# A transpose on one core: part of the second load is shared out unevenly over the DMA engines, and VectorE waits for the last store

## The chip, the cores and the metric

The kernel runs on one core of one Trainium2 chip. The metric is the device time of one execution in microseconds (us); lower is better. Times are medians of several executions. A profile is one further execution, recorded by the hardware profiler; its span runs from the first to the last instruction.

## The reference

The output is the transpose of an 8192 x 8192 matrix of 32-bit floats, 268 MB in and 268 MB out.

```python
def setup_inputs():
    return {
        "x": np.random.randn(8192, 8192).astype(np.float32),
    }

def reference(x: np.ndarray) -> np.ndarray:
    return np.transpose(x)
```

## The kernel before

The input is cut into chunks of P = 128 rows by J = 4096 columns (S = 32 blocks of 128 x 128), 2 MB each: T = 128 chunks, first the 64 of the left half of the columns, then the 64 of the right half. A load (`load(t)`, line 101) brings chunk t into one of NIN = 3 buffers `in0` to `in2`. A row of a chunk is 4096 floats, 16 KB, and goes to one partition. Chunks 0, 1 and 2 are loaded from SyncE's queue before anything else (lines 143 and 144); every later chunk is loaded from ScalarE's queue, chunk t+3 as soon as TensorE has read chunk t.

TensorE transposes the 32 blocks of a chunk against an identity matrix (`transposes(k)`, lines 112 to 123). It writes PSUM in two halves, `ps0` and `ps1`. ScalarE copies half 0 into SBUF and VectorE copies half 1, in pieces of 128 x 512 or longer runs (line 241). A semaphore of each input buffer, `s_ld[k]`, counts 16 for a landed load and one for each of the two copying engines; TensorE waits for 18, takes 18 off and starts the next chunk. So the next chunk starts when it has landed and when both engines have copied the previous one out of PSUM. `go` in the main loop is that semaphore of the next chunk.

The copies collect in nine regions of the tensor `regs` (NREG = 9, 2 MB each). Eight regions fill at a time, each for a group of B = 4 blocks; the windows of the eight groups are staggered, so that in the steady state one region fills up with each chunk and is stored (`store(q, e, t)`, from line 154) as up to 2 MB in one transfer. Stores go out on ScalarE's queue as well: the first with the ordinary call, the others with `wide_dma` (line 25), which writes the access pattern into the instruction as it stands. Where a window runs across the change from the left to the right half of the columns, the store is cut into two pieces. A region that is used again makes the first copy into it wait for the store's semaphore `s_st[r]`. Each store adds 16 to that semaphore.

Program order on each queue sets the order of transfers. ScalarE alternates copies, a store and a load. At the end, `for r in range(NREG)` makes SyncE wait for all nine store semaphores in turn (line 266), after which all engines leave the section together.

Of the kernel before, what the change touches and what calls it, by code (L numbers as in the profile page):

```python
# [8 lines left out]
def physical(ap):  # L9


    t = ap.tensor
    dims = [list(d) for d in ap.ap]
    if len(dims) == 2:
        dims.insert(1, [dims[1][1], 1])
    return mybir.PhysicalAccessPattern(
        ap=dims,
        offset=ap.offset,
        dtype=ap.dtype,
        memref=t.name,  # L20
        memsetref=t.name + "_set",
    )


def wide_dma(nc, eng, queue, out, in_):


    return eng.add_instruction(
        mybir.InstDMACopy(
            mode="Copy",  # L30
            name=nc.get_next_instruction_name(),
            engine=eng.engine,
            ins=[physical(in_)],
            outs=[physical(out)],
            queue=queue,
        )
    )
# [3 lines left out]
def kernel(  # L41
# [13 lines left out]
    nc = tc.nc  # L55
    P = 128
# [8 lines left out]
    NIN = 3  # L65
    NREG = 9
    CH = N // P
    J = S * P

    with tc.tile_critical():  # L70
        nc.alloc_sbuf_tensor("pad", [P, 32], dt)
        ident = nc.alloc_sbuf_tensor("ident", [P, P], dt).ap()
        ins = [nc.alloc_sbuf_tensor(f"in{k}", [P, J], dt).ap() for k in range(NIN)]
        SIZE = B * W * P
# [4 lines left out]
        s_id = nc.alloc_semaphore("s_id")  # L79
        s_ld = [nc.alloc_semaphore(f"s_ld{k}") for k in range(NIN)]  # L80
        s_st = [nc.alloc_semaphore(f"s_st{k}") for k in range(NREG)]
        s_pe = nc.alloc_semaphore("s_pe")
        s_cp = [nc.alloc_semaphore("s_cpa"), nc.alloc_semaphore("s_cpv")]

# [3 lines left out]
            out=ident,  # L88
            in_=ident,
# [8 lines left out]

        chunks = [(s, c) for s in range(M // J) for c in range(CH)]

        def load(t):
            s, c = chunks[t]
            (nc.sync if t < NIN else nc.scalar).dma_start(
                out=ins[t % NIN], in_=x[c * P:(c + 1) * P, s * J:(s + 1) * J]
            ).then_inc(s_ld[t % NIN], 16)

# [34 lines left out]
        for t in range(NIN):  # L143
            load(t)

        copied = [0, 0]
        free = list(range(NREG))
        stored = [0] * NREG
        window = {}

        def later(t):
            return W <= t < T - NIN

        def store(q, e, t):
            t0, r, parts = window.pop(q)
            if later(t):
                nc.scalar.wait_ge(s_pe, (t + 1) * NH + 1)
            else:
                nc.scalar.wait_ge(s_cp[e], copied[e])
            base = 0  # L160
            pieces = []
            for s, a, z in parts:
                rows = (z - a) * P
                j0 = s * J + q * B * P
                dst = out[j0:j0 + B * P, a * P:a * P + rows]
                dst = dst.rearrange("(q b) i -> q b i", q=P)
                src = regs[:, r * SIZE + base:r * SIZE + base + B * rows]
                base += B * rows
                pieces.append((rows, dst, src))
            for rows, dst, src in sorted(pieces, key=lambda v: -v[0]):  # L170
                if any(stored):
                    st = wide_dma(nc, nc.scalar, "qActDynamicHW", dst, src)
                else:
                    st = nc.scalar.dma_start(
                        out=dst, in_=src.rearrange("q (b i) -> q b i", b=B)
                    )
                st.then_inc(s_st[r], 16)
                stored[r] += 1
            free.append(r)

        def closes(w, t):
            t0, r, parts = w
            return t + 1 == t0 + sum(z - a for _, a, z in parts)

        for t, (s, c) in enumerate(chunks):
            closed = []
            for e in range(2):
                eng = (nc.scalar, nc.vector)[e]
                go = s_ld[(t + 1) % NIN]

                place = []
                fresh = {}
                for q in range(e * NH, (e + 1) * NH):
                    if q not in window:

                        span = (q - c) % W + 1
                        r = free.pop(0)
                        parts = [(s, c, min(c + span, CH))]  # L200
                        if c + span > CH and t + span < T:
                            parts.append((s + 1, 0, c + span - CH))
                        window[q] = (t, r, parts)
                        if stored[r]:
                            fresh[q - e * NH] = (s_st[r], 16 * stored[r])
                    t0, r, parts = window[q]
                    k = [p[0] for p in parts].index(s)
                    base = r * SIZE + B * P * sum(z - a for _, a, z in parts[:k])
                    _, a, z = parts[k]
                    place.append((base + (c - a) * P, (z - a) * P))  # L210

                runs = []
                for g in range(NH):
                    if runs:
                        u = runs[-1]
                        gap = place[g][0] - place[g - 1][0]
                        if place[g][1] == place[u[0]][1] and abs(gap) < 2 ** 15 and (
                            len(u) == 1 or gap == place[u[1]][0] - place[u[0]][0]
                        ):
                            u.append(g)  # L220
                            continue
                    runs.append([g])
                if later(t):
                    runs = sorted(runs, key=lambda u: any(g in fresh for g in u))
                seen = t * NH + e * NH // 2
                for u in runs:
                    off, dist = place[u[0]]
                    gap = place[u[-1]][0] - place[u[-2]][0] if len(u) > 1 else 0
                    dims = [list(regs.ap[0]), [gap, len(u)], [dist, B], [1, P]]
                    o = bass.AP(regs.tensor, regs.offset + off, dims)  # L230
                    i = pss[e][:, u[0] * B * P:(u[-1] + 1) * B * P]
                    i = i.rearrange("p (l b i) -> p l b i", b=B, i=P)
                    need = t * NH + (e * NH + u[-1]) // 2 + 1
                    if later(t) and u is runs[0] and len(runs) > 1 and any(g in fresh for g in runs[-1]):
                        need = t * NH + (e * NH + max(v[-1] for v in runs)) // 2 + 1
                    if need > seen:
                        eng.wait_ge(s_pe, need)
                        seen = need
                    for sem, value in [fresh[g] for g in u if g in fresh]:
                        eng.wait_ge(sem, value)  # L240
                    cp = nc.scalar.copy(out=o, in_=i) if e == 0 else nc.vector.tensor_copy(out=o, in_=i)  # L241
                    ends = [e * NH + g for g in u if closes(window[e * NH + g], t)]
                    if later(t):
                        if u is runs[-1]:
                            cp.then_inc(go, 1)
                        closed += [(q, e) for q in ends]
                        continue
                    if ends:
                        cp.then_inc(s_cp[e], 1)
                        copied[e] += 1  # L250
                    if u is runs[-1]:
                        if ends:
                            eng.wait_ge(s_cp[e], copied[e])
                            eng.sem_inc(go, 1)
                        else:
                            cp.then_inc(go, 1)
                    for q in ends:
                        store(q, e, t)
            for q, e in closed:
                store(q, e, t)  # L260
            if t + NIN < T:
                if not closed:
                    nc.scalar.wait_ge(s_pe, (t + 1) * NH)
                load(t + NIN)
        for r in range(NREG):
            nc.sync.wait_ge(s_st[r], 16 * stored[r])


# [28 lines left out]
```

## Time and profile before

| | |
|---|---|
| device time, median of 3 runs | 1261.18 us (1261.06 to 1261.89) |
| span of the profiled execution | 1260.4 us |
| the profiled execution's own time | not recorded apart from its span |
| TensorE, matmul busy | 739.0 us (59%), 4096 instructions |
| VectorE busy | 302.0 us (24%), 250 instructions |
| ScalarE busy | 253.5 us (20%), 257 instructions |
| DMA | 536.95 MB, mean 426 GB/s over the span |
| queue of ScalarE (q10) | 530.60 MB, 99.0% of 16 engines' span |
| queue of SyncE (q1) | 6.29 MB, 1.2% of 16 engines' span |

Busy times say how long an engine computed, not what held the others up. The DMA row counts all bytes read and written by the core's sixteen DMA engines. A window of the trace is a stretch of the span for which the profile gives the granted TensorE clock, the mean busy share of the sixteen DMA engines and the rate in GB/s; a packet is counted in the window in which it starts.

### The profile page before, as it was taken

Reading aid. Unit: us, or ns where it says so; the run is one execution under the profiler, and the core shown is the slowest. Engines: PE = TensorE matmul, PEld = TensorE weight load, DVE = VectorE, ACT = ScalarE, POOL = GpSimd, SP = SyncE. Lnnn points to the kernel's source line nnn. Section 1 sums busy time; section 2 is a strip of 40 time slices with the busy share of each in tenths; the row PEclk is TensorE's granted clock in tenths of the full one; section 3 lists DMA queues with packets and bytes.
Section 4 is the critical chain, followed back from the end, with each engine's and each line's share of the span. In section 5 each row is a group of like instructions: output and inputs, shape, how many; then the busy total and the mean of one; then the engine's idle time right before and its main releaser. Section 6 shows DMA issues by size and latency. Waiting matters only on the chain. (4 is left out here: it accounts for less than half of the span.)

```text
span 1260.4 us, 9367 instructions
## 1 busy us (share of the span) xinstructions
PE 739.0 (59%) x4096; PEld 718.4 (57%) x4096; DVE 302.0 (24%) x250; ACT 253.5 (20%) x257; POOL 0.7 (0%) x6
## 2 busy tenths in 40 slices
PE   5656556565566655565556656566565655665561
PEld 5556556565556655565555656565565655665561
DVE  2322222222222222222222222222222222222220
ACT  3212211122111211122111211121111211121110
POOL 0000000000000000000000000000000000000000
PEclk9886876868777777778687786867777687777776
DMA  9999999999999999999999999999999999999998
GB/s 383 429 422 426 425 430 431 426 431 431 427 430 431 428 428 431 428 429 432 427 422 426 429 429 425 431 429 428 430 428 428 431 428 429 429 429 429 429 431 376
DMA packets 39271, 536.95 MB, mean 426 GB/s; under 512 B 4320, under 2 KB 4832, under 8 KB 6240
## 3 DMA queue, kind: packets, MB, share of 16 engines
q10 hardware_dynamic: 38832, 530.60, 99.0%
q1 hardware_dynamic: 432, 6.29, 1.2%
q14 instruction: 6, 0.05, 0.0%
q8 instruction: 1, 0.02, 0.0%
HBM read 268.44 MB, written 268.44 MB: 426 GB/s over the span
## 5 line engine op out<-in xcount | busy, mean ns | idle before, releaser
L117 PE MATMUL ps<-ident,in 128*128 128x128 f32 x4096 | 739.0, 362 | 493.5 <-PEq L113 493.5
L117 PEld LDWEIGHTS ps<-ident,in 128*128 128x128 f32 x4096 | 718.4, 220 | 513.9 <-issue 513.9
L241 DVE COPY regs<-ps 128x512 f32<-128x512 f32 (+3 forms) x250 | 302.0, 1246 | 932.1 <-PE ps L117 932.1
L241 ACT COPY regs<-ps 128x512 f32<-128x512 f32 (+3 forms) x256 | 252.2, 1016 | 978.8 <-PE ps L117 760.8
L241 ACT ACT_TABLE_LOAD x1 | 1.3, 1283 | 1.0 <-SPq L70 1.0
L87 POOL TENSOR_SCALAR_AFFINE_SELECT ident<-ident 128x128 f32<-128x128 f32 x1 | 0.3, 293 | 0.2 <-POOL ident L85 0.2
L85 POOL MEMSET ident<- 128x128 f32 x1 | 0.2, 204 | 0.5 <-SPq L70 0.5
L281 POOL MEMSET const-bfloat16-1.0<- 128x1 bf16 x1 | 0.1, 102 | 0.0
L281 POOL MEMSET const-uint8-127<- 128x1 uint8 x1 | 0.1, 102 | 0.0
L281 POOL MEMSET const-float32-0.0<- 128x1 f32 x1 | 0.1, 99 | 0.2 <-issue 0.2
L281 POOL MEMSET const-float32-1.0<- 128x1 f32 x1 | 0.1, 99 | 0.0
## 6 DMA issues: line engine op xcount, KB each, us to landing
in<-in_x_dram ACTq DMA_DIRECT2D x125, 2048.0 KB, 16.8
out_dram<-regs ACTq DMA_DIRECT2D x114, 2048.0 KB, 12.6
out_dram<-regs ACTq DMA_DIRECT2D x4, 1792.0 KB, 11.1
in<-in_x_dram SPq DMA_DIRECT2D x3, 2048.0 KB, 11.7
out_dram<-regs ACTq DMA_DIRECT2D x4, 1536.0 KB, 12.5
out_dram<-regs ACTq DMA_DIRECT2D x4, 1280.0 KB, 11.5
out_dram<-regs ACTq DMA_DIRECT2D x4, 1024.0 KB, 11.1
out_dram<-regs ACTq DMA_DIRECT2D x4, 768.0 KB, 12.3
```

The costliest lines, as they stand in the source:

```text
L85: nc.gpsimd.memset(ident, 0.0).then_inc(s_id, 1)
L87: nc.gpsimd.affine_select(out=ident, in_=ident, compare_op=mybir.AluOpType.not_equal, fill=1.0, base=0, pattern=[[-1, P]], channel_multipl ...
L117: tr = nc.tensor.transpose(pss[e][:, (g * B + b) * P:(g * B + b + 1) * P], ins[k][:, q * B * P + b:(q + 1) * B * P - B + b + 1:B], ident,)
L241: cp = nc.scalar.copy(out=o, in_=i) if e == 0 else nc.vector.tensor_copy(out=o, in_=i)
L281: nc = _bacc.Bacc("TRN2", target_bir_lowering=False, num_devices=1)
```

## The change

Chunk 1 is no longer loaded by one transfer. The ordinary load covers its first 112 rows. Two more transfers on SyncE's queue, made with `wide_dma`, bring the other 16: 12 rows viewed as 4 x 3 and 4 rows viewed as 2 x 2. They have a semaphore of their own, `s_ex`, and VectorE waits for 32 on it before its last copy of chunk 0, the one that reports to `s_ld[1]`. At the end of the kernel, the wait for the last region stored, `free[-1]`, is VectorE's; SyncE keeps the other eight.

```diff
     CH = N // P
     J = S * P
+    EXTRA = [(4, 3), (2, 2)]
...
         s_st = [nc.alloc_semaphore(f"s_st{k}") for k in range(NREG)]
+        s_ex = nc.alloc_semaphore("s_ex")
...
         def load(t):
             s, c = chunks[t]
+            src = x[c * P:(c + 1) * P, s * J:(s + 1) * J]
+            a = P - sum(e * n for e, n in EXTRA) if t == 1 else P
             (nc.sync if t < NIN else nc.scalar).dma_start(
-                out=ins[t % NIN], in_=x[c * P:(c + 1) * P, s * J:(s + 1) * J]
+                out=ins[t % NIN][:a], in_=src[:a]
             ).then_inc(s_ld[t % NIN], 16)
+            if t == 1:
+                for e, n in EXTRA:
+                    part = src[a:a + e * n].rearrange("(e n) j -> e n j", e=e)
+                    wide_dma(nc, nc.sync, "qSPDynamicHW", ins[t][a:a + e * n], part).then_inc(s_ex, 16)
+                    a += e * n
...
                     for sem, value in [fresh[g] for g in u if g in fresh]:
                         eng.wait_ge(sem, value)
+                    if t == 0 and e == 1 and u is runs[-1]:
+                        eng.wait_ge(s_ex, 16 * len(EXTRA))
                     cp = nc.scalar.copy(out=o, in_=i) if e == 0 else nc.vector.tensor_copy(out=o, in_=i)
...
         for r in range(NREG):
-            nc.sync.wait_ge(s_st[r], 16 * stored[r])
+            (nc.vector if r == free[-1] else nc.sync).wait_ge(s_st[r], 16 * stored[r])
```

## The prediction

> **What bounds the kernel now.** I read the page first (busy shares, slices, DMA queues), then windows over the start, the middle and the end, then the timeline of the start, the DMA issues and the waits. The page settles the bound:
>
> ```profile
> span 1260.4 us, 9367 instructions
> ## 1 busy us (share of the span) xinstructions
> PE 739.0 (59%) x4096; PEld 718.4 (57%) x4096; DVE 302.0 (24%) x250; ACT 253.5 (20%) x257; POOL 0.7 (0%) x6
> ...
> DMA  9999999999999999999999999999999999999998
> GB/s 383 429 422 426 425 430 431 426 431 431 427 430 431 428 428 431 428 429 432 427 422 426 429 429 425 431 429 428 430 428 428 431 428 429 429 429 429 429 431 376
> ```
>
> No compute engine is above 59%; the DMA engines are at nine tenths or more in every slice but the last. Windows (length, clock, DMA share, GB/s) show how completely they are filled:
>
> ```profile
> 2.00:18.00 16.00, 1.00 0.98 404
> 18.00:24.00 6.00, 1.00 1.03 394
> 24.00:60.00 36.00, 0.91 1.02 430
> 60.00:180.00 120.00, 0.78 1.01 425
> 180.00:600.00 420.00, 0.75 1.01 429
> 600.00:720.00 120.00, 0.73 1.01 426
> ```
>
> A share of 1.01 (packets overlap by a little) at 429 GB/s means that all sixteen engines work back to back: 429/16 = 26.8 GB/s each, and a row of 16 KB (4096 floats) takes 16384 B / 26.8 GB/s = 0.61 us. So the span is the work of the engine that ends last: its start, its packets at 0.61 us, its slow packets, and a tail. Bytes are equal for all sixteen, so what differs between engines is start and slow packets. The end shows by how much, if I cut it into windows of about one packet:
>
> ```profile
> 1255.20:1255.80 0.60, 0.50 1.03 437
> 1255.80:1256.40 0.60, 0.50 0.84 355
> 1256.40:1257.00 0.60, 0.50 0.65 273
> 1257.00:1257.60 0.60, 0.50 0.33 137
> 1257.60:1258.20 0.60, 0.50 0.26 109
> 1258.20:1258.80 0.60, 0.50 0.00 0
> ```
>
> GB/s times 0.6 us over 16384 B is the number of engines that begin a packet in the window: 16, 13, 10, 5, 4, 0. So after 1255.8, 3 engines begin no more packet, 3 begin one, 5 two, 1 three and 4 four. (A slow packet could hide an engine in one window; I take the counts as they are.) Perfect balance would give each 32/16 = 2 packets, so about 2 of them, 1.2 us, are all that sharing out rows could ever win here; a change in the number of slow packets comes on top.
>
> **The change, part by part.**
>
> *Rows.* Of the second load 112 rows remain in the sixteen-way transfer: 7 an engine instead of 8. Then 12 rows go to four engines (3 each) and 4 rows to two (2 each). If both small transfers start at the same engine, two engines carry 7+3+2 = 12 rows (+4), two carry 10 (+2) and twelve carry 7 (-1); bytes are conserved (8+4-12 = 0). As engines never run dry, the difference stays to the end: +2.4 us, +1.2 us and -0.6 us there. With k the packets that an engine begins after 1255.8, the last engine has 4 before; after, the two have k+4, the two others k+2, the rest k-1. The change at the end is then the largest of (k of the two), (k of the two others, minus 2) and -1, in packets. It is never below zero unless the two belong to the earliest three, and there it is about zero. This is the heart of my forecast: on these counts the moved rows can hardly win, since +4 rows uses up the whole spread of 4.
>
> The trace does not say which engines get the small transfers. [...]
>
> Any two of sixteen, drawn blindly, have as the larger k: 0 in 3 pairs of 120, 1 in 12, 2 in 40, 3 in 11, 4 in 54; the mean is (12+80+33+216)/120 = 2.8 packets, 1.7 us. Against a blind draw stands the start:
>
> ```profile
> 2.00:2.25 0.25, 1.00 1.67 328
> 2.25:2.50 0.25, 1.00 0.74 197
> 2.50:2.75 0.25, 1.00 1.13 328
> 2.75:3.00 0.25, 1.00 0.51 197
> ```
>
> By the same sum 5, 3, 5 and 3 engines take up their first packet in these four windows: the engines start one after another over some 0.9 us. If those that are served first are those that the small transfers use, they lead the mean by about 0.4 us, 0.7 packet. 2.8 - 0.7 is 2 packets: **+1.2 us**, with bounds of -0.2 us (the earliest two, and the sub-packet rest in my favour) and +2.4 us (one of the latest four).
>
> *The start: two more issues and a wait.*
>
> ```profile
> 0.94 1.32 SPq L103 DMA_DIRECT2D in<-in_x_dram  x3
> ...
> 12.97 2.48 DVE L241 COPY regs<-ps 128x512 f32<-128x512 f32 x4 [12.97 <-PE ps L117]
> ...
> 15.60 4.11 PE L117 MATMUL ps<-ident,in 128*128 128x128 f32 x32 [1.70 <-PEq L113]
> ...
> 17.95 0.59 ACTq L28 DMA_DIRECT2D out_dram<-regs  x1
> ...
> 19.75 0.34 ACTq L103 DMA_DIRECT2D in<-in_x_dram  x1
> ```
>
> ```profile
> in<-in_x_dram ACTq DMA_DIRECT2D x125, 2048.0 KB, 16.8
> out_dram<-regs ACTq DMA_DIRECT2D x114, 2048.0 KB, 12.6
> ...
> in<-in_x_dram SPq DMA_DIRECT2D x3, 2048.0 KB, 11.7
> ...
> out_dram<-regs ACTq DMA_DIRECT2D x4, 256.0 KB, 12.1
> ```
>
> SyncE issues three loads in 1.32 us, 0.44 us each; the third goes out two issues, 0.9 us, later. A load is 2 MB, 4.9 us at 428 GB/s, so two earlier loads hide that: zero. The second load is issued at 0.94+0.44 = 1.4 us and lands 11.7 us later (the median of three is the second), at 13.1 us. Its last rows now land four rows later, at about 15.5 us. VectorE has to wait for them before the last of its four copies of the first tile, which would start at 12.97 + 3 x 0.62 = 14.8 us: a wait of 0.7 us. Queued behind it are that copy and the signal that lets TensorE take the second tile, so the 15.60 becomes about 16.3, the store of 17.95 goes out at 18.6 and the load of 19.75 at 20.4. Who waits for that? Only the DMA queue: a load needs 4.9 us of transfer and lands 16.8 us after its issue (stores 12.6), so some 7 to 12 us of work stand ahead of each transfer. 0.7 us out of that is hidden: zero. If this cover were gone it would cost 0.7 us once.
>
> *Later in the run* the engine with +4 rows makes each landing up to 3 us later than its neighbours. ScalarE, which issues all transfers, does wait for stores:
>
> ```profile
> ACT regs L241 <- DMA out_dram<-regs: 83.2, 38, 8.5
> ```
>
> Each such wait can grow by up to 3 us, and with it the next issues. That eats 3 of the 7 us of queue and starves at worst the engines that are ahead; the late one, which sets the end, has more queued than they. Zero at the end.
>
> *The tail.*
>
> ```profile
> L266 SPq EVENT_SEMAPHORE  x4: 27/28/4912, 1250.4 to 1254.3; - x4
> ...
> L70 SPq COMPARE_BRANCH  x1: 33/33/33, 1259.2 to 1259.2; - x1
> ...
> L70 DVEq DRAIN  x1: 17/17/17, 1259.4 to 1259.4; - x1
> ```
>
> SyncE waits from 1254.3 for 4.9 us, to 1259.2; then it leaves the section, signals, and 0.2 us after that the other engines drain, VectorE among them. With VectorE waiting for the last store, SyncE has signalled long before and the chain starts at VectorE's drain. [...] I take the row nearest to it, the 0.2 us between branch and drain, as **-0.2 us**, with bounds of -0.2 and +0.2.
>
> **Sum:** +1.2 + 0 + 0 - 0.2 = +1.0 us. The profiled span of 1260.4 would become 1261.4. The times given are 1261.06 to 1261.89, median 1261.18, 0.8 us above that span, which I take as the launch's part and unchanged: 1262.2 us. What a measurement of this kernel can tell from no change is about 0.2%, 2.5 us; the forecast is inside it.
>
> **Rivals.**
>
> A. *The engines that get more are the early ones.* Then nothing is lost and the tail is won: -0.2 to -0.4 us, 1260.9. For it: the staggered start. Against: only 3 to 6 of 16 are early enough.
>
> B. *Fewer slow packets* (faster). At 18 to 24 us the rate is 394 instead of 430, and at 60 to 180 us 425 instead of 429: 6 x 36/430 = 0.5 us and 120 x 4/429 = 1.1 us. If engines collide there because they run in step, moving four of them out of step early could save both: 1.6 us, and with the sixteenth of a load that most engines lose (0.6) and the tail (0.2) about 2.4 us, 1258.8, or a little lower. Against: the rate after 600 falls just as much with the engines long spread out.
>
> C. *Slower than the bound.* If one of the two engines with +4 rows is one of the four latest, the end moves by the full 2.4 us; what decides is a k of 4. If the disturbed start also costs the 0.5 us of 18 to 24 us once more, it is +2.7 us with the tail: 1263.9. For it: 54 of 120 pairs hold such an engine. Against: the dip has to repeat as well.
>
> D. *A small transfer costs its engine a fixed time.* [...] As a mechanism here: the second load's 11.7 us hold two loads, 9.8 us, of transfer; if the 1.9 us left were engine time for each small transfer, two of them would add 3.8 us to the forecast: 1266.0. Against: a 256 KB store lands in 12.1 us, a 2048 KB one in 12.6, both queued; and between 600 and 720 us, where the panel changes and seven stores are cut in two, the rate is 426: 120 x 3/429 = 0.84 us over seven extra stores, 0.12 us each.
>
> E. *The rows do not spread.* If both small transfers ran on one engine, that engine would carry 7+16 = 23 rows, 15 more: 15 x 0.61 = 9.2 us, less the 1.2 us by which a middling engine (2 packets of 4) stands ahead of the last: +8.0 us, 1269.0.
>
> **How the numbers follow.** Forecast (balance +0.4 to +2.4, 1261.4 to 1263.4) 0.60; A 0.14; B 0.09; C 0.12; D 0.02; E 0.03. Of the forecast 0.05 lies beyond +2.5 us through other slow packets; of B 0.06 beyond -2.5. So faster 0.06, slower 0.12 + 0.02 + 0.03 + 0.05 = 0.22, same 0.72. The range runs from 1259.9 (A, and the upper half of B's gain left out) to 1264.0 (C in).
>
> **What would show it.** In the profile after, the windows of one packet at the end should show two engines ending after all others, about 2 packets beyond the place of the last one before, and twelve ending 0.6 us earlier; the DMA share of 1.01 in the middle unchanged; VectorE's first four copies stretched by about 0.7 us and TensorE's second tile at about 16.3 us; SyncE's last wait ending near 1254 us. I am wrong if the last windows close together (A), if the rate at 18 to 24 or 60 to 180 us rises towards 430 (B), if it falls (C), or if a single engine trails by 5 us or more (E).

## The result and the profile after

The changed kernel takes 1276.87 us (median of 5 executions, 1273.81 to 1283.45) against 1261.30 us (1261.06 to 1261.89): ratio 1.0125, 95% interval 1.0104 to 1.0145, 15.6 us slower. The forecast was 1262.2 us, with a range up to 1264.0. The profiled execution is the slowest of the five, 1283.45 us with a span of 1281.7 us; it overstates the median's loss, and the account below is of this execution.

The page of the changed kernel, the lines that answer to those of before:

```profile
span 1281.7 us, 9370 instructions
PE 739.2 (58%) x4096; PEld 718.5 (56%) x4096; DVE 302.0 (24%) x250; ACT 253.5 (20%) x257; POOL 0.7 (0%) x6
...
DMA  9999999999999999999999999999999999999998
GB/s 293 408 430 428 430 430 429 430 428 431 427 430 429 431 427 430 427 431 424 423 417 423 426 420 419 427 419 422 424 424 418 420 420 418 422 418 415 419 409 362
```

The same work on every compute engine, the same nine tenths of DMA share in all slices but the last, and yet a lower rate in two places: the first two slices, and the slices from the nineteenth on. A share that stays while the rate falls means that the engines are busy for longer with each packet, and not that they are idle: the 67 packets that start from 8 to 12 us took 0.81 to 1.17 us, all 107 of the kernel before 0.61 us. Windows of the same kernel (length, clock, DMA share, GB/s) make it plain:

```profile
2.00:18.00 16.00, 1.00 1.02 300
18.00:24.00 6.00, 0.50 0.97 308
24.00:60.00 36.00, 0.89 0.98 391
60.00:180.00 120.00, 0.79 1.01 429
180.00:600.00 420.00, 0.75 1.01 429
600.00:720.00 120.00, 0.73 1.01 422
720.00:1220.00 500.00, 0.76 1.01 420
```

Before, the first three rows had 404, 394 and 430 GB/s, and the last one stood like this:

```profile
720.00:1220.00 500.00, 0.75 1.01 429
```

Over the first 60 us as one window, first the kernel before, then the changed one:

```profile
2.00:60.00 58.00, 0.94 1.01 419
```

```profile
2.00:60.00 58.00, 0.88 0.99 357
```

That is 58 x (419 - 357)/429 = 8.4 us of transfer lost at the start. From 60 to 180 us the rate is 429 instead of 425, and 120 x 4/429 = 1.1 us are won back; from 180 to 600 us nothing changes. From 600 to 720 us it is 120 x (426 - 422)/429 = 1.1 us lost, from 720 to 1220 us 500 x (429 - 420)/429 = 10.5 us. That makes 18.9 us; the other 2.4 of the 21.3 us between the spans fall after 1220 us. So there are two losses, at the start and after 600 us. What the first one is made of stands in the timeline (start, length, instruction, idle time before it and what ended that):

```profile
1.86 1.51 SPq L28 DMA_DIRECT2D in<-in_x_dram  x2
3.41 0.39 SPq L107 DMA_DIRECT2D in<-in_x_dram  x1
...
23.11 0.69 DVE L252 COPY regs<-ps 128x512 f32<-128x512 f32 x1 [6.82 <-DMA in<-in_x_dram]
...
23.94 5.88 PE L126 MATMUL ps<-ident,in 128*128 128x128 f32 x32 [8.49 <-PEq L122]
...
27.04 0.59 ACTq L28 DMA_DIRECT2D out_dram<-regs  x1
...
29.86 0.34 ACTq L107 DMA_DIRECT2D in<-in_x_dram  x1
```

VectorE's fourth copy waits 6.82 us for the two small transfers, until 23.1 us. TensorE's second tile starts at 23.94 us instead of 15.60, the second store and the fifth load go out at 27.04 and 29.86 us instead of 17.95 and 19.75. The rate falls first, between 8 and 20 us, while the share stays above 1; from 28 to 32 us the DMA engines run dry, and the share is well below 1. Three windows of the changed kernel:

```profile
8.00:12.00 4.00, 1.00 1.03 274
12.00:20.00 8.00, 0.87 1.02 233
...
28.00:32.00 4.00, 0.97 0.76 258
```

The same three windows of the kernel before, with which the experiments are compared too:

```profile
8.00:12.00 4.00, 1.00 1.02 438
12.00:20.00 8.00, 1.00 1.00 410
...
28.00:32.00 4.00, 1.00 0.97 409
```

How the two small transfers were spread is told by the times at which the semaphore `s_ex` goes up in the trace: twice right after the issues, at 3.0 and 3.8 us, then four times between 19.0 and 19.7 us and twice at 23.0 and 23.1 us. That fits four engines for the 4 x 3 rows and two for the 2 x 2, one for each step of the outer dimension (`e` in the edits); the engine counts of the experiments are taken from `e` in the same way. At the end (one packet a window) two engines end last:

```profile
1276.80:1277.40 0.60, 0.50 0.58 246
1277.40:1278.00 0.60, 0.50 0.58 246
1278.00:1278.60 0.60, 0.50 0.13 55
1278.60:1279.20 0.60, 0.50 0.13 55
1279.20:1279.80 0.60, 0.50 0.13 55
```

By GB/s times 0.6 us over 16384 B that is nine engines in each of the first two windows and two in each of the last three: two engines end three packets, 1.8 us, after the last seven of the others.

### The profile page after: what moved, and what is told of

It is laid out like the page before. It is cut to its first block, busy times and chain, and to the rows that moved or that the text cites. A ratio compares the mean times of both kernels' runs of the same rounds, so it can differ in the third digit from the quotient of the medians.

```text
span 1281.7 us, 9370 instructions
## 1 busy us (share of the span) xinstructions
PE 739.2 (58%) x4096; PEld 718.5 (56%) x4096; DVE 302.0 (24%) x250; ACT 253.5 (20%) x257; POOL 0.7 (0%) x6
```

## The experiments

Theories for the start: **S**, the 112-row transfer itself is slow; **U**, uneven shares and transfers on four and two engines are slow, and **Q**, any transfer on few engines is slow; later **L**, the place in SBUF, against **H**, the place in HBM. For the part after 600 us: **G**, a spread between the engines that is too large, against **N**, no connection with it. Times are compared with runs of the kernel before on the same chip (its median was 1262.00, 1262.42 and 1261.09 us beside e1 to e4, e5 to e8, and the rest). The rates come from one profiled execution of each kernel.

**e1_vector_wait**, the last wait alone:

```diff
-            nc.sync.wait_ge(s_st[r], 16 * stored[r])
+            (nc.vector if r == free[-1] else nc.sync).wait_ge(s_st[r], 16 * stored[r])
```

> Only the last part of the change: VectorE instead of SyncE waits for the last store; all loads as before. The loss seen in the changed kernel (about 15 us) lies in the first 60 us and after 600 us, so every theory expects none of it here: -0.2 us, at most 0.2 us either way.

1262.21 us against 1262.00 us, ratio 1.0005 (0.9993 to 1.0016): no measurable effect. From the last landing to the end of the span it is 1.16 us, against 1.27 us before: the tail's gain is 0.1 us. The profiled execution was the one of eleven that took 1272.25 us, 10 us above the median of this kernel, and it lost its time where the changed kernel loses its second part:

```profile
720.00:1220.00 500.00, 0.75 1.01 422
```

Its loads are those of the kernel before. So the second loss can come without any change to the loads, here in one execution of eleven; theory G was formed on this.

**e2_one_each**, the changed kernel's 112-row transfer, with the other 16 rows one to an engine (SyncE keeps the final waits):

```diff
-    EXTRA = [(4, 3), (2, 2)]
+    EXTRA = [(16, 1)]
```

> The second load again in 112 rows on sixteen engines (7 each), but the other 16 rows go one to each of sixteen engines: every engine carries 8 rows, as before the change. SyncE keeps all final waits. Theory S (the 112-row transfer itself, seven consecutive rows an engine, is slow, whatever follows it): rate near 280 GB/s at 8 to 14 us, TensorE's second tile at 19 us or later, 3 to 9 us slower than before. Theory U (uneven shares and transfers on four and two engines are slow): rate near 420 GB/s at 8 to 14 us, second tile at 15.6 to 16.5 us, within 1 us of before.

1264.83 us against 1262.00, ratio 1.0029 (1.0015 to 1.0042). Rows of its windows and timeline:

```profile
8.00:12.00 4.00, 1.00 1.07 315
12.00:20.00 8.00, 0.95 0.97 284
...
720.00:1220.00 500.00, 0.74 1.01 430
```

```profile
18.98 5.57 PE L126 MATMUL ps<-ident,in 128*128 128x128 f32 x32 [4.23 <-PEq L122]
```

Shares are even here and the start is slow all the same: 315 and 284 GB/s instead of 438 and 410. S is supported and U alone is not the cause; after 600 us nothing is lost.

**e3_spare**, whole loads, the two small transfers added into a tensor that nobody reads:

```diff
+            if t == 1:
+                a = P - 16
+                for e, n in [(4, 3), (2, 2)]:
+                    part = x[c * P + a:c * P + a + e * n, s * J:s * J + J - 512].rearrange("(e n) j -> e n j", e=e)
+                    wide_dma(nc, nc.sync, "qSPDynamicHW", spare[a:a + e * n], part).then_inc(s_ex, 16)
+                    a += e * n
...
+        nc.sync.wait_ge(s_ex, 32)
         for r in range(NREG):
```

> All loads whole, as before; the two small transfers (12 rows on four engines, 4 rows on two) are added behind the second load and write to a spare tensor that nobody reads, rows of 14 KB instead of 16 (the SBUF has no more room). Two engines carry 4.4 rows' worth more, two 2.6, the rest none, which is the lag of the changed kernel without its 112-row transfer and without its wait. Theory S: rate near 400 GB/s at 2 to 14 us, slower only by the extra work of the late engines, 0.5 to 2.7 us. Theory U: rate below 320 GB/s at 8 to 18 us, and 4 us or more slower. If the rate after 600 us falls to about 420 as in the changed kernel, the lag does it and not the start; 429 would say the other.

1271.09 us (1267.68 to 1278.00), ratio 1.0066 (1.0049 to 1.0083).

```profile
8.00:12.00 4.00, 1.00 1.01 434
12.00:20.00 8.00, 1.00 1.00 272
```

S fails as the whole cause: with whole loads the second one runs at 434 GB/s, but in the window of the small transfers the sixteen engines together fall to 272. The change has two slow parts, and they needed one theory. Of the part after 600 us this run says less than it was to: the rate is 424 from 60 to 600 us and 426 from 720 to 1220, so it falls earlier than in the changed kernel and recovers in part.

**e4_third**, the same split on the third load:

```diff
-            a = P - sum(e * n for e, n in EXTRA) if t == 1 else P
+            a = P - sum(e * n for e, n in EXTRA) if t == 2 else P
...
-                    if t == 0 and e == 1 and u is runs[-1]:
+                    if t == 1 and e == 1 and u is runs[-1]:
```

> The same uneven split, on the third load instead of the second, with VectorE's wait before its last copy of the second tile; SyncE keeps all final waits. Theory S: the second tile starts at 15.6 to 16.5 us as before, packets are slow from 12.5 us on, when the third load runs, and the third tile waits to 26 us or later. If it were only that the second load has no time to spare, the third, with 3 us more, would land its rows by 21.4 us and cost 1 us at most.

One execution, 1273.20 us. The dip moves with the split, and three microseconds more of slack do not help; VectorE's last copy of the second tile waits until 27.5 us:

```profile
8.00:12.00 4.00, 1.00 1.02 438
12.00:20.00 8.00, 1.00 1.04 302
20.00:28.00 8.00, 0.75 0.97 279
```

```profile
27.50 0.69 DVE L252 COPY regs<-ps 128x512 f32<-128x512 f32 x1 [5.98 <-DMA in<-in_x_dram]
```

**e5_own_parts and e6_own_rows**, one extra transfer of 16 rows on four engines, in e6 with source and place exchanged (`[(112, 0)]`); the edit of e5:

```diff
+                for d0, r0 in [(0, 112)]:
+                    part = x[c * P + r0:c * P + r0 + 16, s * J:s * J + J - 512].rearrange("(e n) j -> e n j", e=4)
+                    wide_dma(nc, nc.sync, "qSPDynamicHW", spare[d0:d0 + 16], part).then_inc(s_ex, 16)
```

> All loads whole. Behind the second load one extra transfer: 16 rows of 14 KB, four to each of four engines, from rows 112 to 127 of the chunk into partitions 0 to 15 of a spare tensor, where a whole load's first rows land too. Theory L (the place in SBUF: an engine that writes partitions which another engine writes in the whole loads holds that one up): rate above 390 GB/s at 12 to 20 us, third tile at 21.4 to 22.5 us. Theory H (the place in HBM, rows 112 to 127 read by other engines than usual): rate below 330 GB/s at 12 to 20 us, third tile at 24 us or later. Theory Q (any transfer on few engines is slow): also below 330.

> As the run before it, with source and place exchanged: rows 0 to 15 of the chunk into partitions 112 to 127 of the spare tensor. Theory L: rate below 330 GB/s at 12 to 20 us and third tile at 24 us or later. Theory H: above 390 GB/s and 21.4 to 22.5 us. Theory Q: below 330.

Into partitions 0 to 15 (e5: 1265.56 us, ratio 1.0025, 1.0010 to 1.0040), the window and the third tile:

```profile
12.00:20.00 8.00, 1.00 1.01 405
```

```profile
21.80 4.11 PE L123 MATMUL ps<-ident,in 128*128 128x128 f32 x32 [1.71 <-PEq L119]
```

Into partitions 112 to 127 (e6: one execution, 1266.21 us):

```profile
12.00:20.00 8.00, 1.00 0.98 281
```

```profile
22.84 6.59 PE L123 MATMUL ps<-ident,in 128*128 128x128 f32 x32 [3.25 <-PEq L119]
```

The same number of rows on the same number of engines: 405 GB/s or 281, decided by the partitions they land in and not by the rows they come from. L holds; H and Q fall. (The third tile of e6 came 1 us earlier than L's figure.) L says which split is slow, but not how far it reaches. By L alone the four engines and those that they hold up would be slow here, and yet every one of the 29 packets that start between 14 and 16 us in e6 took 1.13 us or longer, against a median of 0.61 us in the kernel before. So all the engines were slowed; why, no run shows. The dip does not show in the times, 0.65 us apart: e5's profiled execution has more long packets later on (table below).

**e8_halves**, the second load in two transfers of 64 rows, with VectorE's wait for the second of them:

```diff
+            a = P // 2 if t == 1 else P
...
+            if t == 1:
+                nc.sync.dma_start(out=ins[t][a:], in_=src[a:]).then_inc(s_ex, 16)
...
+                    if t == 0 and e == 1 and u is runs[-1]:
+                        eng.wait_ge(s_ex, 16)
```

> The second load in two transfers of 64 rows, each four rows an engine; every engine carries 8 rows as before, nothing else is added. Theory L: with 64 partitions only half of the places are written at a time, so two engines share each: rate near 215 GB/s from 7.7 us until the load has landed, at 17 us or later, second tile at 18 us or later. Theory Q and U: 420 GB/s, second tile at 15.6 to 16.5 us. Theory H has no reason for half the rate: above 300.

One execution, 1265.96 us.

```profile
8.00:12.00 4.00, 1.00 1.00 205
```

```profile
19.39 5.42 PE L122 MATMUL ps<-ident,in 128*128 128x128 f32 x32 [4.81 <-PEq L118]
```

205 GB/s is about half of the 438 that the kernel before has in these four microseconds, as L said. Runs e5, e6 and e8 (405, 281 and 205 GB/s) agree with L. Which engine writes which partitions no trace names, so what holds the engines up there is not shown.

**e7_own_both2, e9_eight_late, e10_eight_half**, a lag without the slow start: extra rows, row r of the chunk into partition r. The edit is that of e5 with another list. e7 has two transfers of 16 rows on four engines, into partitions 0 to 15, where e5 had kept 405 GB/s, and 32 to 47; e9 has two of 32 rows on eight engines (`e=8`), into 0 to 31 and 32 to 63, so that eight engines have eight more rows of 14 KB each, an estimated 4.3 us at 26.8 GB/s an engine. That the start stays fast with these was my estimate; the rates at 12 to 20 us test it. e10 has only the first transfer of e9:

```diff
+                for d0, r0 in [(0, 0), (32, 32)]:
```

> Two extra transfers, rows 0 to 15 into partitions 0 to 15 and rows 32 to 47 into partitions 32 to 47 of the spare tensor: four engines carry eight more rows of 14 KB, 4.3 us, the others none. It gives the lag with as little disturbance of the start as can be had. Theory L and H: rate above 390 GB/s at 12 to 20 us (less the 12 engines' head start); Q: below 330. For the part after 600 us: if a lag of more than 4 us between the engines is what brings the long packets there, the rate falls to about 420 and the time rises by 10 us or more; if not, 429, and the time rises by the lag alone, 2 to 5 us.

> [...] The start is to stay fast (above 390 GB/s at 12 to 20 us). [...] Theory G (a spread of more than 4 us between the engines brings long packets): long packets as soon as the lag is there, rate at 60 to 600 us below 427 against 429, spread of the landings of one transfer 4 to 5.5 us, and 1267 us or more. Theory N (long packets after 600 us have nothing to do with the spread): rate 429 in both parts, time up by the lag alone, 1262 + 4.3 = 1266.5 us or less.

> As the run before it with one of the two extra transfers: eight engines late by 2.1 us, less than the spread that the kernel before had by itself (3.3 us in the first half). Theory G: hardly any long packets before 600 us, rate 429 there, 1263 to 1265 us. Theory N: the same. If long packets come here as often as with 4.3 us, the spread is not what decides.

e7: 1267.19 us, ratio 1.0036 (1.0021 to 1.0050). e9: 1279.35 us, ratio 1.0162 (1.0121 to 1.0203). e10: 1277.40 us, ratio 1.0140 (1.0107 to 1.0173). Windows of e9:

```profile
12.00:20.00 8.00, 1.00 1.00 402
...
60.00:600.00 540.00, 0.74 1.01 428
600.00:720.00 120.00, 0.77 1.01 421
720.00:1220.00 500.00, 0.73 1.01 421
```

and of e10:

```profile
12.00:20.00 8.00, 1.00 0.99 400
...
60.00:600.00 540.00, 0.75 1.01 427
600.00:720.00 120.00, 0.73 1.01 424
720.00:1220.00 500.00, 0.76 1.01 423
```

With the start nearly undisturbed (408 GB/s at 12 to 20 us in e7, 402 in e9 and 400 in e10, against 410) and no compute engine waiting for them, extra rows on eight engines cost 16.3 us (e10) and 18.3 us (e9); the rows themselves are an estimated 2.1 and 4.3 us of that, at 26.8 GB/s an engine. My figures for these runs missed: e7 was to lose 10 us by G and lost 4.8, its lag and little more; e9 was to fall below 427 GB/s from 60 to 600 us and had 428; e10 was to lose 3 at most and lost 16. The size of the lag put in does not decide. The number of late engines goes with it: four rows more on each of four engines (e5) cost 3.1 us, on each of eight (e10) 16.3; eight rows more on four (e7) cost 4.8, on eight (e9) 18.3.

**after2**, the changed kernel once more:

> The changed kernel once more, for a second profile. The start is to repeat: rate near 300 GB/s at 2 to 24 us, second tile at 23 to 25 us, 8 to 10 us lost by 60 us. Theory G: the loss after 600 us varies from execution to execution, and in the profile goes with the spread of the landings of one transfer: about 5 us where the rate is 420 or less, under 4 us where it is 428 or more. If the rate is 420 with a spread under 4 us, G is wrong.

1272.68 us, ratio 1.0084 (1.0064 to 1.0103); profiled span 1273.0 us.

```profile
2.00:60.00 58.00, 0.88 0.98 354
60.00:600.00 540.00, 0.76 1.01 427
600.00:720.00 120.00, 0.75 1.01 422
720.00:1220.00 500.00, 0.75 1.01 429
```

The start repeats: 58 x (419 - 354)/429 = 8.8 us lost. The loss after 720 us is absent this time. What goes with it can be worked out from the completions and packets of all thirteen traces. The spread is the time from the first to the last of the sixteen completions of one load (median of the loads in the stretch, in us). Behind the stroke stands the time by which packets of more than 0.65 us exceeded 0.61 us, in us for each engine. A column is a stretch of the span in us.

```
kernel           60-200    200-400   400-600   660-800   800-1000  1000-1200
before           3.2/1.4   3.5/0.3   3.3/0.4   3.0/0.4   2.8/0.5   2.8/0.3
changed          3.9/0.1   3.8/0.3   4.6/0.5   5.3/2.4   5.3/3.7   5.8/5.4
changed, again   4.1/0.6   4.2/0.5   5.3/3.1   4.1/1.0   2.2/0.4   2.5/0.3
e1               3.7/0.8   3.6/0.2   3.7/0.1   5.2/1.5   5.3/4.0   5.4/4.1
e2               3.5/0.5   3.2/0.3   3.4/0.1   3.8/0.1   3.7/0.1   3.7/0.0
e3               4.4/0.5   5.3/3.6   5.3/4.3   5.3/0.9   5.3/3.1   4.9/1.5
e4               3.5/0.1   3.5/0.1   4.0/0.3   4.6/0.3   4.6/0.9   5.4/3.0
e5               3.4/0.1   3.5/0.1   3.9/0.3   5.2/1.0   5.1/3.2   3.3/0.3
e6               2.9/0.2   3.1/0.1   3.5/0.0   4.1/0.1   4.5/1.1   5.0/0.6
e7               4.8/0.6   5.2/3.0   3.2/1.1   3.2/0.9   2.7/0.2   3.3/0.1
e8               3.5/0.4   3.5/0.4   3.4/0.2   3.7/0.1   3.7/0.0   3.7/0.1
e9               4.3/0.0   4.7/0.8   5.3/1.4   5.9/3.0   5.4/3.7   5.5/4.5
e10              3.3/1.0   4.2/0.0   5.4/2.5   5.3/2.3   4.3/6.2   4.0/0.3
```

Where the median spread is 4.3 us or less, a stretch has 1.4 us or less of long packets, with one exception: e10 at 800 to 1000 us, where 4.5 of the 6.2 us lie before 900 us, while the spread falls from 5.5 to 4.4. From 4.4 to 5.0 us it is 0.3 to 1.5 us; at 5.1 us and more it is 0.9 to 5.4, mostly 2.3 or more. The spread that is put in at the start is not the one that counts, for it grows or shrinks on the way: in e10 from 2.6 us at 52 us to 5.5 us at 510 us, in e7 from 5.2 to 3.2 us. It does not start anew in the stretch from 630 to 700 us, where the stores run across the change from the left to the right half of the columns (the panel of the prediction): the loads there have 3.3 to 3.0 us in the kernel before and 5.2 us or more all the way in the changed kernel and in e10; in e1 they go from 3.7 to 5.2 us. G holds as to what goes together. Which of the two is the cause, and why it starts near 5 us, about the 4.9 us that a load takes at 428 GB/s, stays open; no run here tells it.

## Why the prediction was wrong, step by step

- *What bounds the kernel*: right. The DMA engines set the time before and after; both losses are in them.
- *How the rows are shared out*: right as to the counts. The completions fit four engines and two, and two engines end last. Rival E falls. The twelve others did not end together, 0.6 us early: nine engines run on to 1278.0 us. What the balance cost by itself, put at 1.2 us, cannot be told apart from the rest.
- *A row costs 0.61 us, wherever it lands*: this step failed first. The rate of the changed kernel from 8 to 20 us, 274 and 233 GB/s, makes 0.96 and 1.13 us of a row as a mean of the sixteen engines, and none of the 67 packets that start from 8 to 12 us took less than 0.81 us. I moved rows between engines without asking into which partitions each engine then writes. All loads of the kernel before have one shape, and so one split; 112 rows in sevens and 16 rows on four and two engines split otherwise. That the partitions decide is shown by e5 and e6, 405 and 281 GB/s with the same number of rows and of engines; which partitions each engine writes, in either split, is not shown.
- *The start: an issue is 0.44 us, the wait of VectorE 0.7 us, hidden by the queue*: failed, the wait as a consequence. The two small transfers took 1.51 us to issue, and the third load went out at 3.41 us, 1.6 us later than before instead of 0.9. VectorE's wait was 6.8 us, TensorE's second tile came 8.3 us late, and the queue ran out from 28 to 32 us (share 0.76): (0.97 - 0.76) x 4 = 0.8 us of idle engines. I had priced it at 0.7 us if the cover were gone, but held the cover to be safe.
- *Later in the run: zero*: failed. I held that an engine's lag can only starve those ahead of it, and put the change in slow packets at nothing. e9 and e10, with late engines and hardly a slow start, lost 16 to 18 us, with long packets at a share of 1.01 and not with idle engines. In the profiled execution of the changed kernel the loss from 600 to 1220 us is the larger one, 11.6 of 21.3 us; in after2 it is a few microseconds. That a spread of about 5 us goes with it is shown, that it is the cause is not.
- *The tail, -0.2 us*: right in sign, 0.1 us in size, and by e1 not measurable. No run shows the +0.2 us of its upper bound: the branch of the waiting engine started 0.06 us after the last landing with SyncE (kernel before) and 0.03 us after it with VectorE (changed kernel). The 0.8 us that I took as the launch's part is 1.7 to 1.9 us in every run that has its own span on record; it cancels out of the sum, which adds +1.0 us to a time.
- *Rival D* (a fixed cost of a small transfer) came out slow for the wrong reason: in e5 the small transfer, into partitions 0 to 15, leaves the rate at 405 GB/s against 410. *Rival C* named the dip at the start as what would repeat, priced at 0.5 us; the start cost 8.4. *Rival B*'s sign did show from 60 to 180 us, 429 GB/s instead of 425; but e1, with the loads of before, has 427 there, so part of this is there without the change; and after 600 us the late groups of e9 and e10 had more long packets, where B expected fewer.

No version tried beats the kernel before.

## What to carry to other kernels

Look at a transfer's split over DMA engines together with the partitions that it writes: in this kernel 128 partitions in one transfer kept sixteen engines at 438 GB/s, two transfers of 64 had 205, and 16 extra rows on four engines left 405 of 410 in partitions 0 to 15 and 281 in 112 to 127. Where the DMA engines are the bound, be wary of a lag between groups of them: late by 2.1 or 4.3 us, four engines cost 3 and 5 us in this kernel and eight engines 16 and 18, so a constant offset is not a constant cost. And a wait that is covered by a queue is safe only as long as the price of what is waited for is known from a transfer of the same shape.

## What the runs showed of the hardware that I had not expected

A transfer on four of sixteen engines slowed down all sixteen: 281 GB/s against 410 in e6, while the same in other partitions ran at 405 (e5). Engines that are given equal rows drifted apart: in the kernel before the sixteen completions of a load lie 0.3 us apart at 13 us, 3.2 us at 70 us, and 2.5 to 3.8 us from there to the end. With completions spread over 5.3 to 5.8 us (medians) the rate of the changed kernel went down from 429 to 420 GB/s at an unchanged share of 1.01; the kernel with the loads of before (e1) fell into it by itself in one profiled execution and lost 10 us.
